# A hybrid decoder layer: input phase and output projection in another order, the second weight difference made in another block

## The chip, the core and the metric

The kernel runs on one core of a Trainium2 chip. The metric is the device time of one execution in microseconds (us). A core has five engines with a queue each: TensorE (PE: matmuls and transposes), VectorE (DVE), ScalarE (ACT), GpSimd (POOL) and SyncE (SP, which here issues DMAs). An engine takes its instructions in the order in which they stand in its queue and waits on semaphores for the other engines and for DMAs.

## The reference, cut to what matters

The program is one layer of a decoder trunk with three gated branches. It computes for 1024 prompt rows and 64 sample rows of 1024 columns:

```python
h = rmsnorm(x, g_pre)
proj = h @ w_in                       # 1024 -> 7 * 512 + 3 * 1024 columns
a      = pool_mix(p_in) * silu(p_gate)            # trailing windows, per-group linear
bconv  = silu(layernorm(dwconv31(c_val * sigmoid(c_glu)))) * silu(c_gate)
cattn  = attention(q, mem_k, mem_v) * silu(x_gate)
br     = einsum('bsnw,nwd->bsnd', stack([a, bconv, cattn]), w_branch)
merged = sum_n sigmoid(merge_logits_n) * br_n     # M, transposed, in the kernel
y      = merged @ w_out
x_new  = x + rmsnorm(y, g_post)
```

Beside it, mem_k and mem_v are `rmsnorm(mem_prompt) @ w_mem_kv` for 256 memory tokens.

## The kernel before

**Numbers.** Matmul operands are pairs of float16 tiles, a high part and a low part. `hilo` (L74) makes them: ScalarE writes the high part (L75) and VectorE or POOL the low part (L77 without a scale, L79 with one). `mm3` (L81) multiplies two pairs in three matmuls (L85, L88, L89).

**Blocks.** Big products use a scheme with seven block products in place of eight. The activation's operands are seven blocks in the tile `BO`, each of four K-tiles: B11, B21, B22 and the sums T1 to T4. The weights are loaded into `raw`, combined (s1 to s4) by accumulating DMAs that POOL issues (L499 to L507), and split into `ws`. Products go to PSUM tiles `pm` and `pb`, four of each.

**Input phase.** `startup` (L236) loads and scales x, turns it by TensorE transposes (`flip`, L225, into `pb`), and splits it. The first half gives B11 and B21. `second_half(k)` (L290) turns K-tile k of the second half, makes the differences `tq` (L292, L295), and splits B12, B22 and T1; behind the four of them T2 is split, then POOL makes the sums for T3 and T4 (L312, L313). In between stand the two first products (`first`, L275), which fill the gates `sg0` with a Sigmoid (L280) as each arrives; the memory tokens' root-mean-squares (L169, L156: a Sqrt at L159 and a Newton step on VectorE, `newton`, L141); their scaling (`mem_kv`, L339); the split of the pooling weights (in `states`); and the splits of s1 and s2 of the first column pair (`prep1`, `prep2` of `pair`, L446). A tile scheduler puts the instructions of each engine in order, by its own estimate of when each can run.

**Middle.** A list of stages holds 7-product pairs for the columns of w_in, the convolution's taps (L715), attention, and `merge` (L1123), which writes the rows of M (L1155, L1157). The gates' evictions are L513, L632 and L660.

**Output projection.** M now is the activation and w_out is split into `BO`. Its 1024 x 1024 are four blocks of four tiles: (0, 0) and (0, 1) in `q` tiles, (1, 0) and (1, 1) in `raw` tiles. `wo_negate` is a ScalarE copy in place (L1213), `wo_add` four accumulating DMAs of 256 KB issued by POOL (L1217), `wo_split` four hi/lo splits. A table, which is in the diff below, hangs them on stages. The first difference (0, 1) + (0, 0) with (0, 1) negated is T1. The second is (1, 1) += (0, 1); it gives T2 and overwrites (1, 1), so it waits until (1, 1) has been split into B22. It is then added to (0, 0) and (1, 0) for T3 and T4.

`pair_of` (L585) runs the seven products of an `out_pair` (L1275): its sums of M are made on POOL (L594, tiles `sr`), split into `ws`, and its evictions are L602. `Rows.part` (L1258) takes a finished half of a row tile: a Square with its sum (L1260) and a product with the norm's weight (L1265); at the second half it forms the root (L1264, L159, Newton), scales and adds x (L1272), and stores the rows.

## Time and profile before

| | us |
|---|---|
| runs, median | 916.86 |
| runs, all | 915.79, 916.86, 920.7 |
| profiled execution | 915.45 |
| its span in the trace | 913.7 |
| TensorE / VectorE busy | 852.5 / 693.6 |
| ScalarE / POOL busy | 462.1 / 319.7 |
| mean granted TensorE clock | 0.975 |

The profile is one execution. Its page gives busy times, 40 slices of the span with the busy share of each engine and the granted TensorE clock in tenths, the chain of work that ended last, and groups of instructions by line and by the program's names (`ws<-raw,ws` writes a `ws` tile from a `raw` and a `ws` tile). Views of the trace give windows, waits with the instruction that ended them, and the timeline of an engine.

### The profile page before, as it was taken

What the parts mean: (1) busy time and instruction counts of PE and PEld (TensorE: products, weight loads), DVE (VectorE), ACT (ScalarE), POOL (GpSimd) and SP (SyncE); (2) the same over time, 40 slices, a digit from 0 to 9 for tenths busy, and PEclk for the clock granted to TensorE, in tenths of its full rate; (3) what the DMA queues carried; (4) which work ended last, traced back from release to release, by engine and by line L of the source; (5) the groups of instructions that cost most, each with busy time, mean ns of one, the idle gap of its engine ahead of it and who ended that gap; (6) DMA issues with size and microseconds to landing.
All of it is one profiled execution on the core that took longest, in us unless ns stands there. A gap on an engine that the chain in (4) does not pass through costs nothing. (4 is left out here: it accounts for less than half of the span.)

```text
span 913.7 us, 15151 instructions
## 1 busy us (share of the span) xinstructions
PE 852.5 (93%) x5765; PEld 458.3 (50%) x5765; DVE 693.6 (76%) x1097; ACT 462.1 (51%) x988; POOL 319.7 (35%) x354
## 2 busy tenths in 40 slices
PE   5869989999999889999989989999999999998986
PEld 3325445545555545555444545555545555544532
DVE  4798599999957799999988777555345543669886
ACT  7767546645653533333445544456345434645542
POOL 1454243344343451211333556511133212346500
PEclk8979999999999999999999999999999999997998
DMA  8625742425566324434343435545654658463142
GB/s 303 170 56 156 202 97 47 92 70 116 120 219 170 93 40 102 95 63 99 84 106 85 94 80 119 119 111 109 132 122 104 119 127 244 124 136 86 70 127 92
DMA packets 101540, 107.42 MB, mean 118 GB/s; under 512 B 5486, under 2 KB 72036, under 8 KB 101452
## 3 DMA queue, kind: packets, MB, share of 16 engines
q1 hardware_dynamic: 82748, 68.24, 23.8%
q0 software_dynamic: 18720, 38.22, 23.6%
q8 instruction: 45, 0.74, 0.3%
q14 instruction: 27, 0.22, 0.1%
HBM read 62.37 MB, written 6.33 MB: 75 GB/s over the span
## 5 line engine op out<-in xcount | busy, mean ns | idle before, releaser
L85 PE MATMUL pm<-BO,ws 128*128 128x512 f16 x836 | 317.8, 382 | 10.2 <-ACT h L513 3.2
L88 PE MATMUL pm<-BO,ws 128*128 128x512 f16 x836 | 319.2, 382 | 1.1 <-DVE BO L77 0.6
L89 PE MATMUL pm<-BO,ws 128*128 128x512 f16 x836 | 317.6, 382 | 1.6 <-DVE ws L79 1.6
L79 DVE SCALAR_TENSOR_TENSOR ws<-raw,ws 128x512 f16<-128x512 f32 x228 | 188.0, 841 | 73.7 <-ACT ws L75 71.9
L88 PEld LDWEIGHTS <-ws 128*128 128x128 f16 x1548 | 148.4, 99 | 128.1 <-issue 21.6
L89 PEld LDWEIGHTS <-ws 128*128 128x128 f16 x1548 | 148.6, 98 | 121.1 <-issue 5.5
L85 PEld LDWEIGHTS <-ws 128*128 128x128 f16 x1548 | 148.1, 99 | 115.2 <-issue 6.9
L75 ACT ACTIVATE ws<-raw 128x512 f16<-128x512 f32 x228 | 137.8, 628 | 126.8 <-PE pm L89 47.7
L715 DVE SCALAR_TENSOR_TENSOR q<-q,cw,q 128x1024 f32<-128x1024 f32 x120 | 167.8, 1407 | 4.0 <-ACT q L712 3.7
L85 PE MATMUL pb<-q,ws 128*128 128x364 f16 (+1 forms) x288 | 92.4, 322 | 2.0 <-DVE q L1155 2.0
L88 PE MATMUL pb<-q,ws 128*128 128x364 f16 (+1 forms) x288 | 92.5, 321 | 0.0
L89 PE MATMUL pb<-q,ws 128*128 128x364 f16 (+1 forms) x288 | 92.5, 321 | 0.0
L499 POOL DMA_DIRECT2D raw<-raw x25 | 21.9, 877 | 198.3 <-ACT raw L498 182.5
L513 ACT ACTIVATE h<-pm 128x512 f32<-128x512 f32 x75 | 44.2, 591 | 49.4 <-PE pm L89 49.3
L1155 DVE SCALAR_TENSOR_TENSOR q<-q,pb 128x364 f32<-128x364 f32 (+1 forms) x72 | 37.3, 526 | 32.7 <-PE pb L89 27.8
L466 DVE SCALAR_TENSOR_TENSOR q<-pm,h 128x512 f32<-128x512 f32 x51 | 34.9, 685 | 29.8 <-PE pm L89 12.8
L506 POOL DMA_DIRECT2D raw<-raw x25 | 21.6, 863 | 75.7 <-DVE ws L79 26.4
L75 ACT ACTIVATE q<-q 128x1024 f16<-128x1024 f32 (+2 forms) x37 | 35.3, 970 | 24.5 <-DVE q L869 10.9
L77 POOL TENSOR_TENSOR q<-q,q 128x1024 f16<-128x1024 f32 (+1 forms) x17 | 36.8, 2175 | 25.8 <-ACT q L75 25.8
L498 ACT ACTIVATE raw<-raw 128x512 f32<-128x512 f32 x50 | 31.0, 625 | 28.7 <-DVE ws L79 28.1
L507 POOL DMA_DIRECT2D raw<-raw x25 | 22.0, 882 | 66.6 <-DVE ws L79 22.1
L85 PE MATMUL pm<-BS,ws 128*128 128x64 f16 x416 | 43.0, 193 | 1.5 <-DVE q L466 1.5
(240 smaller groups left out, 1252.6 us busy)
## 6 DMA issues: line engine op xcount, KB each, us to landing
raw<-in_w_in SPq DMA_DIRECT2D x104, 256.0 KB, 2.9
raw<-raw POOLq DMA_DIRECT2D x104, 256.0 KB, 3.4
q<-in_x_prompt SPq DMA_DIRECT2D x16, 512.0 KB, 9.1
q<-q POOLq DMA_DIRECT2D x14, 544.0 KB, 6.5
raw<-in_w_branch SPq DMA_DIRECT2D x24, 256.0 KB, 3.9
...
```

The costliest lines, as they stand in the source:

```text
L75: nc.scalar.activation(hi, src, AF.Copy, scale=scale)
L77: (eng or nc.vector).tensor_tensor(lo, src, hi, ALU.subtract)
L79: nc.vector.scalar_tensor_tensor(lo, src, scale, hi, ALU.mult, ALU.subtract)
L85: ins = nc.tensor.matmul(out, wh, xh, start=start and j == 0, stop=False, skip_group_check=partial)
L88: nc.tensor.matmul(out, wh, xl, start=False, stop=False, skip_group_check=partial)
L89: nc.tensor.matmul(out, wl, xh, start=False, stop=stop and j == n - 1, skip_group_check=partial)
L466: nc.vector.scalar_tensor_tensor(dst, ps, sc, base, ALU.mult, ALU.add)
L498: nc.scalar.activation(A(1, kh), A(1, kh), AF.Copy, scale=-1.0)
L507: nc.gpsimd.dma_start(out=A(0, 1), in_=A(0, 0), accum_op=ALU.add)
L513: nc.scalar.activation(v[name], ps, AF.Copy, scale=sc)
L715: ins = nc.vector.scalar_tensor_tensor(acc, src, wj, acc, ALU.mult, ALU.add)
L1155: nc.vector.scalar_tensor_tensor(g, g, 1.0, p, ALU.add, ALU.mult)
```

## The change

In the input phase the gates are written with a plain Copy, and one Sigmoid over all 1088 columns of each follows at the end. The memory tokens' squares and roots stay where they were, the rest of their norm is queued behind the last T1 split (`queued`, which hands that split's two instructions to the scheduler as ones to issue after). So are the pooling weights' split and the splits of s1 and s2 of the first pair. `second_half(1)` now stands ahead of `first(1, 0)`.

For w_out the second difference is made in (0, 1): (0, 1) += (1, 1), from stage 4 on, T2 comes from (0, 1), and (0, 1) is added to (0, 0) at stage 6 and to (1, 0) at stage 7. In the row ends, the part behind the second half of a tile becomes `Rows.end`, which is called after the next block's part, and for the last at the end.

```diff
@@ -153,10 +155,16 @@
         nc.vector.scalar_tensor_tensor(r, r, sc, t, ALU.mult, ALU.mult)
         return r
 
-    def rstd_of(ss, inv_n, sc=1.0):
+    def root_of(ss, inv_n):
         p, n = ss.shape
         s = tiny([P, n])[:p]
         nc.scalar.activation(s, ss, AF.Sqrt, scale=inv_n, bias=eps[:p])
+        return s
+
+    def rstd_of(ss, inv_n, sc=1.0, s=None):
+        p, n = ss.shape
+        if s is None:
+            s = root_of(ss, inv_n)
         v = tiny([P, n])[:p]
         nc.vector.tensor_scalar(v, ss, inv_n, EPS, ALU.mult, ALU.add)
         return newton(s, v, (p, n), sc)
@@ -166,11 +174,23 @@
         (eng or nc.sync).dma_start(out=x[:rows], in_=src)
         return x[:rows]
 
-    def rstds(xs):
+    def squares(xs):
         ss = tiny([P, len(xs)])[: xs[0].shape[0]]
         for t, x in enumerate(xs):
             nc.scalar.activation(junk[: x.shape[0]], x, AF.Square, accum_out=ss[:, t : t + 1])
-        return rstd_of(ss, 1.0 / D)
+        return ss
+
+    def rstds(xs):
+        return rstd_of(squares(xs), 1.0 / D)
+
+    behind = []
+
+    def queued():
+
+        es_ = contextlib.ExitStack()
+        for ins in behind:
+            es_.enter_context(tc.issue_after(ins.ins))
+        return es_
 
     BO = cst.tile([P, 7, 2, 4, HALF], F16, name="BO")
     junk = BO[:, 6].rearrange("p a k n -> p (a k n)")[:, : 2 * D].bitcast(F32)
@@ -269,7 +289,8 @@
                 rs_.append(rstds(xt[k + 1 - k // 4 * 2 : k + 3 - k // 4 * 2]))
 
         xs_r = rstds([xs])
-        mem["r"] = rstds(mems)
+        mem["ss"] = squares(mems)
+        mem["s"] = root_of(mem["ss"], 1.0 / D)
         sg0.update({r: Q([P, T]) for r in range(2)})
 
         def first(r, t0, ops):
@@ -277,7 +298,7 @@
             for kh in range(2):
                 w, n = w0[2 * kh + r], ops[kh]
                 mm3(p, [(w[:, 0, k, :], w[:, 1, k, :], n(k)[0], n(k)[1]) for k in range(4)], kh == 0, kh == 1)
-            nc.scalar.activation(sg0[r][:, t0 : t0 + HALF], p, AF.Sigmoid, scale=1.0 / WS)
+            nc.scalar.activation(sg0[r][:, t0 : t0 + HALF], p, AF.Copy, scale=1.0 / WS)
 
         first(0, 0, [lambda k: bo(B11, k), lambda k: bo(B21, k)])
         scale_x(xt[4:6], rs_[0], True)
@@ -294,15 +315,19 @@
             p, gk = flip(k + 4, 1)
             nc.vector.scalar_tensor_tensor(tq[k][:, 1], p, gk, tq[k][:, 0], ALU.mult, ALU.subtract)
             hilo(p, *bo(B22, k), gk)
-            hilo(tq[k][:, 0], *bo(T1, k), -1.0)
+            hi, lo = bo(T1, k)
+            a = nc.scalar.activation(hi, tq[k][:, 0], AF.Copy, scale=-1.0)
+            return a, nc.vector.scalar_tensor_tensor(lo, tq[k][:, 0], -1.0, hi, ALU.mult, ALU.subtract)
 
         second_half(0)
         yield
+        second_half(1)
+        yield
         first(1, 0, [lambda k: bo(B11, k), lambda k: bo(B21, k)])
+        second_half(2)
         yield
-        for k in range(1, 4):
-            second_half(k)
-            yield
+        behind.extend(second_half(3))
+        yield
         for k in range(4):
             hilo(tq[k][:, 1], *bo(T2, k), -1.0)
         for r in range(2):
@@ -329,12 +354,15 @@
             for kh in range(2):
                 w = w0[2 * kh + r]
                 mm3(p[:, r * NS : (r + 1) * NS], [(w[:, 0, k, :], w[:, 1, k, :], BS[:, 0, 4 * kh + k, :], BS[:, 1, 4 * kh + k, :]) for k in range(4)], kh == 0, kh == 1)
-            nc.scalar.activation(sg0[r][:, S:], p[:, r * NS : (r + 1) * NS], AF.Sigmoid, scale=1.0 / WS)
+            nc.scalar.activation(sg0[r][:, S:], p[:, r * NS : (r + 1) * NS], AF.Copy, scale=1.0 / WS)
+            nc.scalar.activation(sg0[r], sg0[r], AF.Sigmoid)
 
     def mem_kv():
         memT = [Q([P, 2, KT // 2, NMEM], F16) for _ in range(2)]
+        with queued():
+            mem["r"] = rstd_of(mem["ss"], 1.0 / D, s=mem["s"])
         for t, m in enumerate(mems):
             nc.vector.tensor_scalar(m, m, mem["r"][:, t : t + 1], None, ALU.mult)
 
@@ -424,7 +452,8 @@
         for g, win in enumerate(WINS):
             for j in range(win - 1):
                 nc.gpsimd.memset(corr[:, g, j : j + 1], float(win) / (j + 1))
-        hilo(pwr, pws[:, 0], pws[:, 1], WS)
+        with queued():
+            hilo(pwr, pws[:, 0], pws[:, 1], WS)
         yield
         nc.sync.dma_start(out=o["conv_s"][0][:, : CB - DS, :], in_=i["state_conv"][0][:, DS:, :])
         nc.sync.dma_start(out=o["pool_s"][0][:, : PB - DS, :], in_=i["state_pool"][0][:, DS:, :])
@@ -473,9 +502,11 @@
                 prep_a11()
 
         def prep1():
-            spl("s1", lambda: v["s1"])
+            with queued() if ahead else contextlib.nullcontext():
+                spl("s1", lambda: v["s1"])
         def prep2():
-            spl("s2", lambda: v["s2"])
+            with queued() if ahead else contextlib.nullcontext():
+                spl("s2", lambda: v["s2"])
         def prep3():
             spl("a12", lambda: A(0, 1))
 
@@ -1222,10 +1253,10 @@
         (-1, lambda: wo_negate(0, 1)),
         (0, lambda: (wo_add((0, 1), (0, 0)), wo_split(B11, 0, 0))),
         (2, lambda: (wo_split(T1, 0, 1, -1), wo_negate(0, 0))),
-        (5, lambda: (wo_split(B21, 1, 0), wo_negate(1, 0))),
-        (6, lambda: (wo_split(B22, 1, 1), wo_add((1, 1), (0, 1)))),
-        (7, lambda: (wo_split(T2, 1, 1), wo_add((0, 0), (1, 1)))),
-        (9, lambda: (wo_split(T3, 0, 0), wo_add((1, 0), (1, 1)))),
+        (4, lambda: (wo_add((0, 1), (1, 1)), wo_split(B21, 1, 0), wo_negate(1, 0))),
+        (6, lambda: (wo_split(B22, 1, 1), wo_add((0, 0), (0, 1)))),
+        (7, lambda: (wo_split(T2, 0, 1), wo_add((1, 0), (0, 1)))),
+        (9, lambda: wo_split(T3, 0, 0)),
         (10, lambda: wo_split(T4, 1, 0, -1)),
     ]:
         stages[last_pair + s][4].append(f)
@@ -1248,6 +1279,12 @@
                 xo[tt] = x_of(tt)
         return f
 
+    ended = []
+
+    def end_rows():
+        while ended:
+            ended.pop(0)()
+
     class Rows:
 
@@ -1259,13 +1296,15 @@
             m, cs = self.m, slice(hf_ * W, (hf_ + 1) * W)
             nc.scalar.activation(half()[:m], ap, AF.Square, scale=sc, accum_out=self.ss[:, hf_ : hf_ + 1])
             self.halves += 1
+            nc.vector.scalar_tensor_tensor(self.y[:, cs], ap, sc, gp[0][:m, cs], ALU.mult, ALU.mult)
             if self.halves == 2:
-                st = tiny([P, 1])[:m]
-                nc.vector.tensor_tensor(st, self.ss[:, 0:1], self.ss[:, 1:2], ALU.add)
-            nc.vector.scalar_tensor_tensor(self.y[:, cs], ap, sc, gp[0][:m, cs], ALU.mult, ALU.mult)
-            if self.halves < 2:
-                return
-            rr, tt = rstd_of(st, 1.0 / D), self.tt
+                ended.append(self.end)
+
+        def end(self):
+            m, tt = self.m, self.tt
+            st = tiny([P, 1])[:m]
+            nc.vector.tensor_tensor(st, self.ss[:, 0:1], self.ss[:, 1:2], ALU.add)
+            rr = rstd_of(st, 1.0 / D)
             dst = o["y_p"][0, tt * P : tt * P + m, :] if tt < S // P else o["y_s"].rearrange("b s d -> (b s) d")
             for hf_ in range(2):
                 cs = slice(hf_ * W, (hf_ + 1) * W)
@@ -1284,7 +1323,11 @@
             return of(r).y[:, c0 : c0 + HALF]
 
         def block(r, c0, ap, scale):
+            mine = ended[:]
             of(r).part(c0 // HALF, ap, scale or 1.0)
+            for f in mine:
+                ended.remove(f)
+                f()
 
         pair_of(lambda r, kh: [M[4 * kh + k][:, (t + 4 * r) * P : (t + 4 * r + 1) * P] for k in range(4)],
                 dest, block, t == 0)
@@ -1327,6 +1370,7 @@
     after(samples_turn)
     out_pair(2)
     out_pair(3)
+    after(end_rows)
     at = len(stages) - 29
     for s, tts in ((-1, (0, 4)), (5, (8,)), (7, (1, 5)), (14, (2, 6)), (21, (3, 7))):
         stages[at + s][4].append(load_x(*tts))
```

Lines of the changed kernel stand further down: L79 becomes L81, L77 becomes L79, L292 L313, L339 L367, L594 L625, L602 L633, L1161 L1192, L1217 L1248, L1264 L1306, L1265 L1299, L1272 L1311.

VectorE in the input phase, the order before, from the scaling of the sample rows on. `t_279` is the memory tokens' root, `q_104` and `q_106` the tokens, `ws_648` to `ws_663` weight splits:

```order
L79 SCALAR_TENSOR_TENSOR ws_648<-raw_126,ws_648 128x512
L79 SCALAR_TENSOR_TENSOR ws_651<-raw_642,ws_651 128x512
L79 SCALAR_TENSOR_TENSOR ws_654<-raw_645,ws_654 128x512
L292 SCALAR_TENSOR_TENSOR q_328<-pb_332,g_pre,q_136 128x512
L145 RECIPROCAL t_283<-t_279 128x2
L295 SCALAR_TENSOR_TENSOR q_328<-pb_340,g_pre,q_328 128x512
L150 TENSOR_TENSOR t_285<-t_283 128x2
L79 SCALAR_TENSOR_TENSOR q_326<-pb_332,g_pre,q_326 128x512
L151 TENSOR_TENSOR t_285<-t_285,t_281 128x2
L79 SCALAR_TENSOR_TENSOR BO<-q_328,BO 128x512
L152 TENSOR_SCALAR t_285<-t_285 128x2
L292 SCALAR_TENSOR_TENSOR q_329<-pb_394,g_pre,q_137 128x512
```

The same place in the order of the change, where `q_319` and `q_320` are the differences of K-tiles 0 and 1:

```order
L313 SCALAR_TENSOR_TENSOR q_319<-pb_323,g_pre,q_136 128x512
L316 SCALAR_TENSOR_TENSOR q_319<-pb_331,g_pre,q_319 128x512
L313 SCALAR_TENSOR_TENSOR q_320<-pb_341,g_pre,q_137 128x512
L81 SCALAR_TENSOR_TENSOR q_317<-pb_323,g_pre,q_317 128x512
L320 SCALAR_TENSOR_TENSOR BO<-q_319,BO 128x512
L316 SCALAR_TENSOR_TENSOR q_320<-pb_349,g_pre,q_320 128x512
L81 SCALAR_TENSOR_TENSOR BO<-pb_331,g_pre,BO 128x512
```

Three weight splits and the Newton step have gone from between the differences, and the second flip's difference follows the first one's at once. The weight splits and the Newton step now stand behind the last T1 split, and the tokens' scaling behind the T3 and T4 low parts.

POOL at the output projection, the order before, from the second sum of M on (`q_7984`, `q_8000`, `q_8019`, `q_8039` hold the K-tiles of blocks (0, 0) and (0, 1) of w_out, `raw_8060` to `raw_8139` those of (1, 0) and (1, 1)):

```order
L594 TENSOR_TENSOR sr_8372<-sr_8367,q_3277 128x128
L594 TENSOR_TENSOR sr_8401<-q_4006,sr_8372 128x128
L594 TENSOR_TENSOR sr_8401<-q_4027,sr_8372 128x128
L594 TENSOR_TENSOR sr_8436<-q_3225 128x128
L594 TENSOR_TENSOR sr_8436<-q_3277 128x128
L594 TENSOR_TENSOR sr_8436<-q_3704 128x128
L594 TENSOR_TENSOR sr_8436<-q_3728 128x128
L1217 DMA raw_8060<-q_7984 128x512
L1217 DMA raw_8090<-q_8000 128x512
L1217 DMA raw_8106<-q_8019 128x512
L1217 DMA q_7984<-raw_8060 128x512
L1217 DMA raw_8060<-raw_8060 128x512
```

The same place in the change, with tile numbers higher by two:

```order
L625 TENSOR_TENSOR sr_8374<-sr_8369,q_3279 128x128
L1248 DMA q_7986<-raw_8062 128x512
L1248 DMA q_8002<-raw_8092 128x512
L1248 DMA q_8021<-raw_8108 128x512
L1248 DMA q_7986<-q_7986 128x512
L1248 DMA q_8041<-raw_8141 128x512
L1248 DMA q_8002<-q_8002 128x512
L625 TENSOR_TENSOR sr_8403<-q_4008,sr_8374 128x128
L625 TENSOR_TENSOR sr_8403<-q_4029,sr_8374 128x128
L1248 DMA q_8021<-q_8021 128x512
L625 TENSOR_TENSOR sr_8438<-q_3227 128x128
```

The second difference now stands directly behind that sum, ahead of six others, and all twelve transfers stand ahead of the later sums.

VectorE within the second pair of row tiles, before. L1264, L161, L145 and L148 to L153 are the root of a finished row tile, `h_9245` a block's combination:

```order
L148 SCALAR_TENSOR_TENSOR t_9153<-t_9151,t_9149 128x1
L1272 SCALAR_TENSOR_TENSOR q_9027<-q_9027,t_9105,q_8932 128x512 x2
L152 TENSOR_SCALAR t_9153<-t_9153 128x1
L1265 SCALAR_TENSOR_TENSOR q_9161<-pb_9163,q_8421 64x512
L1264 TENSOR_TENSOR t_9178<-t_9162 64x1
L1265 SCALAR_TENSOR_TENSOR q_9161<-pb_9171,q_8421 64x512
L153 SCALAR_TENSOR_TENSOR t_9151<-t_9151,t_9153 128x1
L602 SCALAR_TENSOR_TENSOR h_9245<-pm_9232,h_9221 128x512
```

And in the change, where `h_9215` is that combination:

```order
L1299 SCALAR_TENSOR_TENSOR q_9147<-pb_9149,q_8423 64x512
L1299 SCALAR_TENSOR_TENSOR q_9147<-pb_9157,q_8423 64x512
L155 SCALAR_TENSOR_TENSOR t_9137<-t_9137,t_9139 128x1
L633 SCALAR_TENSOR_TENSOR h_9215<-pm_9202,h_9191 128x512
L81 SCALAR_TENSOR_TENSOR ws_9486<-sr_9345,ws_9486 128x128 x4
L1311 SCALAR_TENSOR_TENSOR q_9013<-q_9013,t_9137,q_8918 128x512 x2
```

The scaling of the finished rows has moved from ahead of the combination to behind it.

More of the change, by code (lines that the diff above doesn't have):

```diff
@@ L2 @@
+import contextlib
 import concourse.bass as bass
```

## The prediction

> **What bounds the kernel now.** First the page's engine line and its slices. TensorE is busy 93% of the span, so its own work is the floor, and only what it loses can be won.
>
> ```profile
> PE 852.5 (93%) x5765; PEld 458.3 (50%) x5765; DVE 693.6 (76%) x1097; ACT 462.1 (51%) x988; POOL 319.7 (35%) x354
> ...
> PE   5869989999999889999989989999999999998986
> ...
> PEclk8979999999999999999999999999999999997998
> ```
>
> A slice is 22.8 us. The dips to read are the third slice (46 to 69 us, clock 7) and the 37th (822 to 845, clock 7). The first lies in the input phase, the second at the start of the output projection, where the change works. The windows view in steps of 5 us gives the loss there. Its columns are length, then busy time and count on PE, PEld, DVE, ACT and POOL, then granted clock, DMA share, GB/s.
>
> ```profile
> 40.00:45.00 5.00, 1.50 (x7) 0.68 (x7) 2.93 (x7) 4.96 (x8) 2.82 (x4) 0.97 0.50 91
> 45.00:50.00 5.00, 2.60 (x9) 1.26 (x8) 5.00 (x7) 4.72 (x10) 3.12 (x3) 0.50 0.62 136
> 50.00:55.00 5.00, 3.74 (x14) 1.30 (x13) 5.00 (x6) 1.72 (x3) 2.13 (x3) 0.84 0.54 117
> 55.00:60.00 5.00, 2.21 (x8) 0.83 (x8) 5.00 (x7) 2.07 (x4) 2.78 (x2) 0.84 0.11 20
> 60.00:65.00 5.00, 4.11 (x16) 1.61 (x14) 5.00 (x8) 4.55 (x9) 2.97 (x2) 0.50 0.01 2
> ```
>
> ```profile
> 820.00:825.00 5.00, 2.24 (x8) 0.74 (x6) 3.11 (x5) 1.48 (x4) 2.56 (x6) 0.80 1.08 278
> 825.00:830.00 5.00, 2.90 (x20) 1.20 (x18) 5.00 (x6) 2.88 (x7) 5.00 (x11) 0.84 1.06 216
> 830.00:835.00 5.00, 4.15 (x41) 2.76 (x42) 5.00 (x12) 3.66 (x14) 2.81 (x7) 0.50 0.04 7
> 835.00:840.00 5.00, 5.00 (x76) 3.34 (x74) 4.04 (x17) 3.76 (x19) 0.63 (x2) 0.84 0.02 3
> ```
>
> Busy time times clock is the work at full clock. From 40 to 65 us that is 1.46 + 1.30 + 3.14 + 1.86 + 2.06 = 9.8 us in 25: **15.2 us are lost**. From 820 to 840 it is 1.79 + 2.44 + 2.08 + 4.20 = 10.5 in 20: **9.5 us are lost**. From 45 to 65 us VectorE (DVE) is busy all of 20 us: it makes the operands that TensorE waits for. In the second stall the DMA share is above 1 until 830 us, and VectorE and ScalarE are not full at first: there transfers bound.
>
> The page's rule on its clock is borne out by these rows: 830 to 835 us has 83% of busy time at clock 0.50, after 10 us half idle. The Trainium skill ("TensorE: Matmul & The Clock Gate", "What's actually happening") says that an idle window of about 3.4 us halves the clock and a busy one of that length restores it. By it, a stall that is only cut into small gaps would keep the half clock; that is weighed with the rivals.
>
> **The input phase.** The timeline view shows what VectorE spends there on work that nothing near it needs (start, length, engine, line, operation, and idle time before it with its releaser).
>
> ```profile
> 39.12 0.60 ACT L280 ACTIVATE q<-pm 128x512 f32<-128x512 f32 x1
> 39.74 1.28 ACT L159 ACT_TABLE_LOAD   x1
> ```
>
> ```profile
> 41.36 0.17 DVE L145 RECIPROCAL t<-t 128x2 f32<-128x2 f32 x1 [2.00 <-ACT t L159]
> ...
> 44.31 3.01 DVE L152 TENSOR_SCALAR t<-t 128x2 f32<-128x2 f32 x1
> ...
> 49.88 1.40 DVE L339 TENSOR_SCALAR q<-q,t 128x1024 f32<-128x1024 f32 x2
> 51.21 1.28 DVE L79 SCALAR_TENSOR_TENSOR ws<-raw,ws 128x512 f16<-128x512 f32 x2
> ...
> 67.21 1.75 DVE L79 SCALAR_TENSOR_TENSOR pws<-q,pws 128x512 f16<-128x512 f32 x1
> ...
> 70.45 1.75 DVE L77 TENSOR_TENSOR BO<-h,BO 128x512 f16<-128x512 f32 x1
> ```
>
> Moved behind the operands' splits are: the wait for the memory tokens' root behind table loads (2.00); that Newton chain (five operations, of 0.17 and about 0.15, about 0.75; the 3.01 is a collision, priced below); the memory scaling (1.40); two weight splits (1.28); the pooling weights' split (0.68 alone, by the mean of such splits below). Sum 2.00 + 0.75 + 1.40 + 1.28 + 0.68 = **6.1 us** by which VectorE reaches the last T2 split (70.45) earlier. The two flips that now stand together give it work at once, so I take the whole. The three ScalarE table loads become one with the deferred sigmoids; beyond the 2.00 I cost this at nothing: ScalarE is 2.07 and 1.72 busy in two of the 5 us windows. If that cover were gone the two new sigmoids over 1088 columns, by the 0.60 of one over 512 some 1.3 each, would cost up to 2.6.
>
> What is moved must still be done:
>
> ```profile
> 80.00:85.00 5.00, 5.00 (x72) 3.08 (x69) 2.23 (x5) 1.98 (x5) 0.89 (x2) 1.00 0.95 285
> ```
>
> Here VectorE has 2.77 us free and the moved 4.1 us (6.1 less the wait) do not quite fit; the first split of the next pair (s3) and the memory transposes come late. I take 1.0 back, between nothing and 4.1. **Net 5.1.**
>
> The unknown is contention of VectorE with POOL (GpSimd), shown by groups of the same operation. First POOL and VectorE from 43 to 74 us, last VectorE from 786 to 806 us, where POOL scarcely computes beside it (count, then busy us and mean ns).
>
> ```profile
> L77 POOL TENSOR_TENSOR BO<-h,BO 128x512 f16<-128x512 f32 x4 | 6.2, 1555 | 3.8 <-ACT BO L75 3.8
> L312 POOL TENSOR_TENSOR h<-q,q 128x512 f32<-128x512 f32 x4 | 6.2, 1545 | 0.2
> L313 POOL TENSOR_TENSOR h<-q,q 128x512 f32<-128x512 f32 x4 | 5.7, 1432 | 1.7 <-PE pb L1345 1.0 <-DVE BO L77 0.6
> ```
>
> ```profile
> L79 DVE SCALAR_TENSOR_TENSOR BO<-q,BO 128x512 f16<-128x512 f32 x8 | 9.1, 1134 | 0.0
> L77 DVE TENSOR_TENSOR BO<-h,BO 128x512 f16<-128x512 f32 x4 | 5.2, 1290 | 0.0
> ```
>
> ```profile
> L79 DVE SCALAR_TENSOR_TENSOR BO<-q,BO 128x512 f16<-128x512 f32 x4 | 2.7, 688 | 0.7 <-ACT BO L75 0.7
> ```
>
> The excess is 8 x (1.13 - 0.69) = 3.6, 4 x (1.29 - 0.69) = 2.4, 2.9 on the 0.15 of the Newton operation, and 1.1 on the pooling split: **10.0 us** beside 18.1 us of POOL work. The change leaves these twelve POOL operations as they are, so I keep 10.0. The ends: all 18.1 block, which costs 8.1 more and makes the part 5.1 - 8.1 = -3.0; or as few collide as let it gain 9.
>
> The Trainium skill ("SBUF: State Buffer", "Who interferes with whom") speaks against the change here: a VectorE operation with two SBUF inputs and a POOL operation that reads SBUF shut each other out for their whole length. The rows agree in kind (1134 against 688 ns). By it a denser VectorE row would meet more of the 18.1 us, up to the end of -3.0.
>
> **The output projection.** The timeline of TensorE, POOL, VectorE (the last row of M) and ScalarE, then the landing times of the accumulating transfers (L1217), then windows ahead of the stall:
>
> ```profile
> 823.00 0.21 PE L85 MATMUL pb<-ws,BO 128*128 128x64 f16 x1 [2.76 <-ACT ws L75]
> ```
>
> ```profile
> 789.99 0.46 POOL L594 TENSOR_TENSOR sr<-sr,q 128x128 f32<-128x128 f32 x1
> ...
> 807.17 2.68 POOL L1217 DMA_DIRECT2D raw<-q  x3 [11.77 <-DVE BO L79]
> ...
> 822.44 0.88 POOL L1217 DMA_DIRECT2D q<-raw  x1 [3.56 <-DMA raw<-q]
> ```
>
> ```profile
> 817.66 0.52 DVE L1157 TENSOR_TENSOR q<-q,q 128x360 f32<-128x360 f32 x1
> ```
>
> ```profile
> 831.55 0.63 ACT L75 ACTIVATE BO<-raw 128x512 f16<-128x512 f32 x1 [0.29 <-DMA raw<-raw]
> ```
>
> ```profile
> DMA to landing us min/median/max: 3.2/7.9/13.6
> ```
>
> ```profile
> 790.00:795.00 5.00, 5.00 (x71) 3.55 (x70) 4.01 (x7) 4.52 (x10) 4.50 (x7) 1.00 0.30 106
> 795.00:800.00 5.00, 5.00 (x30) 2.72 (x28) 3.99 (x14) 4.28 (x17) 0.40 (x1) 1.00 0.00 0
> 800.00:805.00 5.00, 5.00 (x28) 2.55 (x27) 0.15 (x2) 1.04 (x4) 0.00 (x0) 1.00 0.00 0
> ```
>
> POOL stands 11.77 us until block (1,1) has been split into B22, since that block is then overwritten. From 807.17 to the last landing's split on ScalarE at 831.55 the twelve transfers take 24.4 us beside the loads of x. The sums of M (L594) are queued behind the waiting transfer of 822.44 on POOL, TensorE waits for those sums' splits, and ScalarE, in order, for each landing.
>
> In the new order the first of the twelve stands right behind the sum that ran at 789.99 before, since block (0,1) is free once T1 is split. So the chain starts some 16 us earlier, in a stretch whose DMA share is 0.30, 0.00 and 0.00. Even with three dependent rounds at the median of 7.9 it ends near 790.5 + 23.7 = 814, before TensorE runs dry at 820. The count of transfers is the same, so nothing is added. What is late next: the M sums now stand behind more transfers, and the last M row is there only at 817.66 as before. I leave 3.0 of the 9.5 for that, bounded by nothing left (gain 9.5) and by a longer wait than now (loss, below). **Gain 6.5.**
>
> **The row ends.** Here TensorE waits 2.69 us for a combination (L602) that stands behind the scaling of finished rows.
>
> ```profile
> 879.17 0.38 PE L85 MATMUL pm<-BO,ws 128*128 128x512 f16 x1 [2.69 <-DVE t L161]
> ```
>
> ```profile
> 875.73 1.41 DVE L1272 SCALAR_TENSOR_TENSOR q<-q,t,q 128x512 f32<-128x512 f32 x2
> ...
> 904.91 0.15 DVE L145 RECIPROCAL t<-t 128x1 f32<-128x1 f32 x1
> ```
>
> With the end of a row queued behind the next block, the 1.41 us and its small Newton operations go from in front of that combination, others take their place: I take **1.0**, between 0 and 2.7. At the very end nothing hides the deferral: three Newton operations of 0.15 now follow the last combination: **-0.5**, between 0 and -1.
>
> **Sum.** 5.1 + 6.5 + 1.0 - 0.5 = 12.1. The profiled execution took 915.45 us (span 913.7), so 903.35; the runs' median, 916.86, is 1.4 above it, and half of that puts the forecast at **904.0**. Its own range is 898 to 908.5. In the long middle, from 130 to 530 us, both queues are shuffled a little; that is 2 or 3 us of unknown sign, inside this range.
>
> **The rivals.** One half per cent (4.6 us) is about what a measurement of this kernel can tell from no change.
> - The denser VectorE queue collides with POOL so that the input phase gains nothing: 915.45 - 6.5 - 1.0 + 0.5 = 908.45. For it the 10.0 us of excess, against it the unchanged twelve operations. 0.13.
> - The output stall only breaks into gaps and TensorE stays at half clock. A stretch such as 825 to 835, with work 2.44 + 2.08 = 4.5 at 7.05 busy, loses 2.5 to the clock alone; with two such stretches and 2 to 3 idle the part gains only 2: 915.45 - 5.1 - 2 - 1.0 + 0.5 = 907.85. For it the 0.50 at 830 to 835. 0.12. It is the result that the rule of the Trainium skill's page "TensorE: Matmul & The Clock Gate" would give for a stall in pieces.
> - The change doesn't do what it says: both stalls are moved, not removed, since TensorE does the same work and VectorE, full at both ends, ends last anyway: 911 to 920. 0.15.
> - Slower, by one mechanism: ScalarE works in order, and the splits of T2 and T3 now stand at about 795 us ahead of the evictions (L513) and gates (L660) that free TensorE's PSUM tiles. If landings need the maximum of 13.6 us in two rounds, to 790.5 + 27 = 817, ScalarE is held, TensorE idles in the merge some 17 us less the 9.5 that it would have lost later, and loses 3 more to half clock while it refills: 915.45 - 4.1 (other parts, input phase at 3.6) + 7.5 + 3 = 922. It decides from landings over about 10 us; against it, the free DMA queues at 795 to 805. 0.06.
> - Better than 898, both parts near their upper ends (9 and 9.5): 0.04.
>
> The forecast keeps 0.50. Faster by over 0.5% means under 912.3: 0.50 + 0.13 + 0.12 + 0.04 and 0.03 of the third rival, 0.82. Within: the rest of that rival, 0.12. Slower: 0.06. The range 897 to 915 leaves out the 0.06, about 0.08 of the third rival above 915 and most of the 0.04.
>
> **What would show it.** In the changed profile: no root wait of 2 us on VectorE near 41 us, the last T2 split near 64 us in place of 70.45, and work at full clock from 40 to 65 near 15 in place of 9.8. POOL's first second-difference transfer near 791 in place of 807, ScalarE's last T4 split before 820 in place of 831.55, and the loss from 820 to 840 (shifted by the earlier gain) near 3. The wait of 2.69 near 879 under 2. Wrong would be: mean split times above 1134 ns at the start; idle TensorE between 790 and 815; clock 0.5 in the output projection's first 10 us.

## The result and the profile after

The changed kernel took **903.88 us** (median of four runs, 900.14 to 904.58); the kernel before took 916.33 us beside it (913.23 to 920.7). The ratio is **0.9856, with a 95% interval of 0.9826 to 0.9886**. The profiled execution took 903.34 us with a span of 901.6. The forecast was 904.0. The total was right, but several of its terms were not: the row ends came out three times their size, the w_out part gave nothing beside the others, and a stretch priced at nothing gave as much as the input phase.

First the changed kernel's page: busy time of the engine, then the slices of TensorE and of its granted clock.

```profile
PE 847.4 (94%) x5765; PEld 456.8 (51%) x5765; DVE 688.4 (76%) x1097; ACT 462.4 (51%) x988; POOL 314.0 (35%) x354
...
PE   5979999999999879899999989999999999898995
...
PEclk8889999999999989999999999999999999999998
```

A slice is 22.5 us now. Both dips that the prediction named, at slices 3 and 37, are shallower, but a new one stands at slice 35 (766 to 789 us), just ahead of the old second dip. The windows view of the changed kernel (length, busy time and count on PE, PEld, DVE, ACT and POOL, granted clock, DMA share, GB/s), input phase first:

```profile
25.00:30.00 5.00, 4.48 (x11) 1.57 (x11) 5.00 (x10) 2.82 (x5) 1.48 (x1) 0.50 0.84 232
...
40.00:45.00 5.00, 5.00 (x28) 2.79 (x27) 5.00 (x6) 1.96 (x4) 3.81 (x4) 1.00 0.30 53
45.00:50.00 5.00, 2.65 (x17) 1.53 (x15) 3.73 (x6) 2.87 (x7) 4.46 (x4) 1.00 0.69 154
50.00:55.00 5.00, 3.07 (x14) 1.38 (x13) 5.00 (x8) 4.80 (x10) 2.42 (x2) 0.55 0.00 0
55.00:60.00 5.00, 5.00 (x20) 2.09 (x19) 5.00 (x8) 4.47 (x9) 3.69 (x3) 0.76 0.01 2
60.00:65.00 5.00, 4.22 (x23) 2.03 (x22) 5.00 (x9) 2.27 (x5) 2.81 (x4) 1.00 0.01 3
65.00:70.00 5.00, 3.53 (x37) 1.89 (x36) 4.89 (x11) 3.08 (x7) 2.10 (x3) 1.00 0.42 75
```

Busy time times clock is again the work at full clock. From 40 to 65 us it is 5.00 + 2.65 + 1.69 + 3.80 + 4.22 = 17.4 us in place of 9.8. To 70 us the loss is 9.1, where it was 15.3 (the 15.2 of the prediction, which ends at 65 us, and 0.1 more). But from 25 to 30 us TensorE now runs 4.48 us at clock 0.50, so 2.8 are lost in this execution. The kernel before lost nothing there:

```profile
25.00:30.00 5.00, 5.00 (x25) 2.16 (x23) 5.00 (x10) 2.73 (x6) 1.84 (x2) 1.00 0.78 246
```

The same view of the changed kernel at the output projection:

```profile
785.00:790.00 5.00, 2.25 (x14) 1.15 (x12) 2.04 (x3) 3.99 (x9) 3.91 (x7) 1.00 0.86 155
...
800.00:805.00 5.00, 3.79 (x21) 1.85 (x19) 1.79 (x4) 2.15 (x6) 0.00 (x0) 1.00 0.59 145
...
810.00:815.00 5.00, 4.02 (x31) 2.00 (x30) 5.00 (x18) 0.63 (x2) 1.91 (x4) 1.00 0.09 35
815.00:820.00 5.00, 2.77 (x17) 0.89 (x14) 4.31 (x13) 2.38 (x10) 4.00 (x7) 0.85 0.00 0
820.00:825.00 5.00, 4.41 (x47) 2.33 (x46) 5.00 (x14) 2.77 (x14) 3.78 (x9) 0.81 0.01 2
```

The losses are 2.75, 1.21, 0.98, 2.65 and 1.43, **9.0 us, against 9.5 before**. They have moved, and they have hardly shrunk. Why the first of them is there is read in two engines' timelines (start, length, engine, line, operation, and in brackets the idle time before it with its releaser). TensorE of the changed kernel:

```profile
788.85 0.38 PE L87 MATMUL pm<-BO,ws 128*128 128x512 f16 x1 [2.75 <-ACT h L544]
```

ScalarE of the changed kernel, at the same time and later:

```profile
785.89 0.63 ACT L77 ACTIVATE BO<-q 128x512 f16<-128x512 f32 x1 [3.06 <-DMA q<-raw]
786.42 0.61 ACT L691 ACTIVATE q<-q 128x512 f32<-128x512 f32 x1
787.16 0.63 ACT L77 ACTIVATE BO<-q 128x512 f16<-128x512 f32 x1
787.70 0.61 ACT L1244 ACTIVATE raw<-raw 128x512 f32<-128x512 f32 x1
788.22 0.58 ACT L544 ACTIVATE h<-pm 128x512 f32<-128x512 f32 x1
...
802.85 0.63 ACT L77 ACTIVATE BO<-raw 128x512 f16<-128x512 f32 x1 [3.33 <-DMA raw<-q]
...
806.54 0.62 ACT L77 ACTIVATE BO<-raw 128x512 f16<-128x512 f32 x1
...
815.95 0.70 ACT L77 ACTIVATE ws<-q 128x128 f16<-128x128 f32 x2 [5.33 <-DVE q L1188]
```

TensorE needs a free PSUM tile for its products. The eviction that frees it (L544) stands four places behind a split of T2 that waits 3.06 us for an accumulating transfer. ScalarE takes its queue in order, so the eviction waits for a landing with which it has nothing to do. This is the "slower" rival's mechanism, at 2.75 us of TensorE. The row at 802.85 does the same through VectorE: its low part of that split waits 3.21 us for the high part, the row of M queued behind it (L1186) comes late, and TensorE idles 1.21 us for that row at 804.71. The last row shown is the other loss: ScalarE stands 5.33 us until a row of M is there, 9 us after the last T4 split (806.54).

To follow where the time goes, the same instruction is compared between two traces: by how many us does each eviction start earlier than in the profiled execution before? Columns are times in the trace of before; the evictions of `pm` into `h` are taken up to 798 us, the combinations of the out pairs behind that (the last at 905).

| kernel | 115 | 249 | 372 | 407 | 483 | 784 | 798 | 837 | 905 |
|---|---|---|---|---|---|---|---|---|---|
| the change | 3.8 | 9.5 | 10.9 | 5.5 | 11.8 | 10.3 | 3.2 | 14.0 | 12.7 |
| e1: input phase alone | 5.7 | 11.5 | 12.7 | 7.3 | 13.7 | 12.0 | 11.8 | 14.0 | 13.2 |
| e2: w_out alone | -1.2 | -0.8 | -1.3 | -1.3 | -1.4 | -2.2 | -8.6 | 2.1 | 0.1 |
| e3: row ends alone | -1.2 | -1.2 | -2.7 | -2.7 | -3.2 | -3.5 | -4.3 | -2.6 | -0.1 |
| e8: input phase, row ends | 4.3 | 10.3 | 11.4 | 6.1 | 12.6 | 11.8 | 10.9 | 13.2 | 16.2 |
| e9: the change, evictions first | 5.2 | 10.4 | 11.6 | 6.3 | 12.7 | 11.2 | 11.4 | 16.9 | 17.6 |

e2 and e3 have before's program until about 760 us and still lie 1.2 to 3.5 behind it: so far do two single traces differ by themselves. The change's lead falls from 10.3 to 3.2 between 784 and 798 us, while M is merged, and rises again where the old stall stood. e1 keeps its 12.0 there. TensorE itself loses only 4.2 us from 785 to 805 by the windows, so part of this fall is the late place of that one eviction and not lost time.

### The profile page after: what moved, and what is told of

Same layout as the page of the kernel before. It is cut to its first block, busy times and chain, and to the rows that moved or that the text cites. A ratio compares the mean times of both kernels' runs of the same rounds, so it can differ in the third digit from the quotient of the medians.

```text
span 901.6 us, 15160 instructions
## 1 busy us (share of the span) xinstructions
PE 847.4 (94%) x5765; PEld 456.8 (51%) x5765; DVE 688.4 (76%) x1097; ACT 462.4 (51%) x988; POOL 314.0 (35%) x354
## 4 chain that ended last, share of the span: by engine, by line
PE 36%; DVE 6%; DMA 4%; POOL 2%; issue 2%; ACT 1%; DVEq 0%; POOLq 0%; ACTq 0%
PE pm L87 9%; PE pm L91 9%; PE pm L90 9%; PE pb L90 3%; PE pb L91 3%; PE pb L87 3%; DVE ws L81 2%; DMA q<-q 1%; DMA raw<-raw 1%; DMA raw<-q 1%; POOL q L1248 1%; DVE q L1311 1%; POOL sr L625 1%; POOL q L1024 0%; DVE BO L81 0%
## 5 line engine op out<-in xcount | busy, mean ns | idle before, releaser
L87 PE MATMUL pm<-BO,ws 128*128 128x512 f16 x836 | 319.1, 383 | 11.6 <-ACT h L544 5.9
L81 DVE SCALAR_TENSOR_TENSOR ws<-raw,ws 128x512 f16<-128x512 f32 x228 | 189.3, 846 | 64.7 <-ACT ws L77 62.9
L77 ACT ACTIVATE ws<-raw 128x512 f16<-128x512 f32 x228 | 138.4, 626 | 120.5 <-PE pm L91 50.3
L746 DVE SCALAR_TENSOR_TENSOR q<-q,cw,q 128x1024 f32<-128x1024 f32 x120 | 165.2, 1383 | 5.5 <-ACT q L743 5.1
L544 ACT ACTIVATE h<-pm 128x512 f32<-128x512 f32 x75 | 44.2, 591 | 56.2 <-PE pm L91 56.1
L1186 DVE SCALAR_TENSOR_TENSOR q<-q,pb 128x364 f32<-128x364 f32 (+1 forms) x72 | 37.1, 526 | 26.3 <-PE pb L91 26.3
L77 ACT ACTIVATE q<-q 128x1024 f16<-128x1024 f32 (+2 forms) x37 | 35.5, 975 | 27.2 <-DVE q L900 13.5
L87 PE MATMUL pm<-BS,ws 128*128 128x64 f16 x416 | 43.7, 193 | 3.1 <-DVE q L495 3.1
L90 PE MATMUL pm<-BS,ws 128*128 128x64 f16 x416 | 43.4, 193 | 1.3 <-DVE BS L79 1.3
```

Of the source, the lines that this page charges most:

```text
L77: nc.scalar.activation(hi, src, AF.Copy, scale=scale)
L81: nc.vector.scalar_tensor_tensor(lo, src, scale, hi, ALU.mult, ALU.subtract)
L87: ins = nc.tensor.matmul(out, wh, xh, start=start and j == 0, stop=False, skip_group_check=partial)
L90: nc.tensor.matmul(out, wh, xl, start=False, stop=False, skip_group_check=partial)
L544: nc.scalar.activation(v[name], ps, AF.Copy, scale=sc)
L746: ins = nc.vector.scalar_tensor_tensor(acc, src, wj, acc, ALU.mult, ALU.add)
```

## The experiments

All ratios are to the kernel before in the same session, with a 95% interval.

**e1, e2, e3: each part alone.** e1 is the change with the old table for w_out and the old row ends. e2 is the kernel before with the new table, e3 the kernel before with `Rows.end`:

```diff
 e1, against the change
-        (4, lambda: (wo_add((0, 1), (1, 1)), wo_split(B21, 1, 0), wo_negate(1, 0))),
+        (5, lambda: (wo_split(B21, 1, 0), wo_negate(1, 0))),
...
-            if self.halves == 2:
-                ended.append(self.end)
 e2, against before
-        (6, lambda: (wo_split(B22, 1, 1), wo_add((1, 1), (0, 1)))),
+        (4, lambda: (wo_add((0, 1), (1, 1)), wo_split(B21, 1, 0), wo_negate(1, 0))),
...
 e3, against before
+            if self.halves == 2:
+                ended.append(self.end)
```

> Only the input phase of the change; output projection and row ends as before. By the prediction's terms: 5.1 us faster, all of it won between 40 and 75 us. By the account made from the two traces (the same evictions, L513, set side by side: 3.8 us ahead at 115 us, 8.9 at 250 to 330, 10.3 from 585 to 784): about 10 us faster, with over half of it won in the middle, from 130 to 540 us, by another order there.

> Only the second difference of w_out in the other block. By the prediction's term: 6.5 us faster. By the traces' account (the lead goes from 10.3 us ahead of the output projection to about 12.9 at the first row tiles behind it): 2 to 3 us faster, with TensorE idle some 2.8 us before an eviction (L513) near 799 us and still losing 4 to 5 us at full clock between 820 and 840.

> Only the row ends deferred. By the prediction's terms: 0.5 us faster (1.0 won near 879, 0.5 lost at the end). By the traces' account: the wait of 2.69 us near 879 is gone, but its gain is given back between 855 and 870, so from 0 to 1 us faster, and a tail about 0.5 us longer behind the last matmul. Rival: 2.2 us faster, the whole wait less the tail.

e1 took 905.58 us, 0.9877 [0.9847, 0.9906]: 11.3 us gained, twice the 5.1 of the prediction. e2 took 912.31, 0.9959 [0.9935, 0.9982]: 3.7 us, between 1.7 and 6.0. e3 took 914.05, 0.9965 [0.9943, 0.9986]: 3.2 us, between 1.3 and 5.2. In e2, without any input phase edit, TensorE waits in the merge for an eviction as in the change:

```profile
800.65 0.41 PE L85 MATMUL pm<-BO,ws 128*128 128x512 f16 x1 [1.99 <-ACT h L513]
```

**e4: the change once more**, as it is, in the session of e1 to e3.

> The changed kernel once more, as the sum to hold the parts against, and for a second profile of it. If the parts are independent its gain is the sum of the other three: 12.1 us by the prediction's terms (5.1 + 6.5 + 0.5), about 12 to 13 by the traces' account (10 + 2.5 + 0 to 1). If the clock of 0.50 from 20 to 30 us in the first profile belongs to one execution and not to the order of the work, this profile shows a clock as before there (0.58, then 1.00).

903.59 us, 0.9849 [0.9819, 0.9879], a gain of 13.9. The three parts alone add up to 18.2, so some 4 us of them are lost together. The second question has its answer too: in e4 the clock is 0.97 from 25 to 30 us, with 3.36 us busy, so 1.7 are lost there and not 2.8. The half clock in that window belongs to one execution; the rest, idle time of TensorE, belongs to the order. The last section shows the rows.

**e5: two taps back.** In the pooling step of the middle, two convolution taps on VectorE stood between three operations that lead to a product. In the input phase's new order the scheduler places them elsewhere, though no edit touches them. e5 is e1 with these two taps tied into their old place:

```diff
+                n = len(taps)
+                with tc.issue_after(mixed[n - 110].ins) if 110 <= n < 112 else contextlib.nullcontext():
+                    ins = nc.vector.scalar_tensor_tensor(acc, src, wj, acc, ALU.mult, ALU.add)
+                taps.append(ins)
```

> The input-phase part alone (as in e1), with two of the convolution's taps put back where they stand before the change, between the three VectorE steps of the first pooling group near 450 us; five rows of VectorE's order and two of ScalarE's differ from e1, nothing else. If the unexpected gain in the middle is those two taps, TensorE idles 1.3 and 2.1 us there again with half clock after it: 4 to 5 us slower than e1, the loss from 440 to 470 us about 6 in place of 0.7. Rival, the gain there comes from elsewhere: no slower than e1 by more than 1 us.

VectorE before (L715 are the taps, L998, L999 and L77 the steps), then TensorE, which waits for the last of them:

```profile
458.04 0.43 DVE L998 TENSOR_TENSOR q<-q,corr 128x1 f32<-128x1 f32 x1 [3.00 <-POOL q L993]
...
458.62 1.28 DVE L715 SCALAR_TENSOR_TENSOR q<-q,cw,q 128x1024 f32<-128x1024 f32 x1
459.81 1.22 DVE L999 SCALAR_TENSOR_TENSOR q<-q,q 128x1024 f32<-128x1024 f32 x1
...
461.55 1.28 DVE L715 SCALAR_TENSOR_TENSOR q<-q,cw,q 128x1024 f32<-128x1024 f32 x1
463.35 1.22 DVE L77 TENSOR_TENSOR q<-q,q 128x1024 f16<-128x1024 f32 x1
```

```profile
464.62 0.46 PE L88 MATMUL pb<-q,pws 128*128 128x364 f16 x1 [2.07 <-DVE q L77]
```

The same place in the changed kernel, VectorE (the steps L1030 and L79, with no tap between them) and then TensorE:

```profile
450.76 1.22 DVE L1030 SCALAR_TENSOR_TENSOR q<-q,q 128x1024 f32<-128x1024 f32 x1
...
453.16 1.23 DVE L79 TENSOR_TENSOR q<-q,q 128x1024 f16<-128x1024 f32 x1
```

```profile
454.44 0.31 PE L90 MATMUL pb<-q,pws 128*128 128x364 f16 x1 [0.84 <-DVE q L79]
```

And in e5, TensorE with the taps back:

```profile
456.49 0.31 PE L90 MATMUL pb<-q,pws 128*128 128x364 f16 x1 [2.20 <-DVE q L79]
```

The wait of 2 us is back. Between 440 and 470 us e5 loses 4.0 us of work at full clock, where e1 loses 0.7 and the kernel before 5.5. e5 took 908.23 us, 0.9918 [0.9889, 0.9947], so 2.7 more than e1 by the medians, 3.8 by the ratios, whose intervals still touch, and 3.3 by the traces. That is less than the 4 to 5 us expected, but far from the rival's 1. Two taps out of 120 are worth more than half of the 5.1 that was given to the whole input phase.

**e6: evictions ahead of the T2 and T3 splits.** The change, with these splits tied behind the last eviction of the merge:

```diff
+            kepts.append(nc.scalar.activation(v[name], ps, AF.Copy, scale=sc))
...
+    def wo_split_late(n, kh, ch):
+        with tc.issue_after(kepts[-1].ins):
+            wo_split(n, kh, ch)
...
-        (7, lambda: (wo_split(T2, 0, 1), wo_add((1, 0), (0, 1)))),
-        (9, lambda: wo_split(T3, 0, 0)),
+        (7, lambda: (wo_split_late(T2, 0, 1), wo_add((1, 0), (0, 1)))),
+        (9, lambda: wo_split_late(T3, 0, 0)),
```

> The changed kernel with the splits of T2 and T3 of w_out queued on ScalarE behind the last pair's evictions (L544). If ScalarE, held by the landing of the second difference ahead of these evictions, is what idles TensorE 2.75 us at 788.85 us, that idle is gone and the kernel is 2 to 3 us faster than the changed one (e4). Rival, the end of M sets the start of the output projection anyway: the idle is gone at 788 and comes back between 810 and 825, and the time is that of e4 within 1 us.

903.02 us, 0.9858 [0.9829, 0.9886]: no gain over the change. The idle is gone at 788 us, as both forecasts said, but it came back at 791, which neither said. So these splits alone don't cost the time. ScalarE and TensorE of e6 show why:

```profile
791.35 0.71 ACT L77 ACTIVATE ws<-sr 128x128 f16<-128x128 f32 x2 [4.93 <-POOL sr L626]
...
794.04 0.57 ACT L545 ACTIVATE h<-pm 128x512 f32<-128x512 f32 x1
```

```profile
794.67 0.38 PE L87 MATMUL pm<-BO,ws 128*128 128x512 f16 x1 [3.36 <-ACT h L545]
```

The next item in ScalarE's queue took the place of the first. It is the split of a sum of M, which POOL makes behind the transfers that were moved ahead of it.

**e7, e10, e11: pieces of the input phase.** Each is e1 with one piece undone: nothing queued (Newton step, pooling weights and weight splits in their old places), the sigmoids in place, `first(1, 0)` ahead of `second_half(1)`:

```diff
 e7
-        with queued():
-            hilo(pwr, pws[:, 0], pws[:, 1], WS)
+        hilo(pwr, pws[:, 0], pws[:, 1], WS)
...
 e10
-            nc.scalar.activation(sg0[r][:, t0 : t0 + HALF], p, AF.Copy, scale=1.0 / WS)
+            nc.scalar.activation(sg0[r][:, t0 : t0 + HALF], p, AF.Sigmoid, scale=1.0 / WS)
...
 e11
+        first(1, 0, [lambda k: bo(B11, k), lambda k: bo(B21, k)])
+        yield
         second_half(1)
         yield
-        first(1, 0, [lambda k: bo(B11, k), lambda k: bo(B21, k)])
```

> The input-phase part without its queueing behind the last T1 split: the sigmoids deferred and the second flip ahead, but the Newton step, the scaling, the pooling split and the pair's splits where the scheduler puts them; from 310 us on VectorE's order is that of before. By the prediction's terms only the 2.0 of the wait for the root is won in the input phase. The stall at 460 us stays (about 6 us lost from 440 to 470). So 2 to 5 us faster than before, against about 11 for e1. Rival, the queueing is worth nothing and the order in the middle all: input phase as in e1 (5 to 6 us ahead at 115 us).

> The input-phase part with each Sigmoid in its old place (three table loads on ScalarE near 35 to 45 us again), flips and queueing as in e1. The prediction puts 2.0 of its 6.1 us on the wait behind those loads: then about 2 us slower than e1, the lead at 115 us (L513) about 2.4 in place of 4 to 5.7. Rival: with the Newton step queued behind the T1 splits nothing near waits for the root, and the loads are hidden: within 1 us of e1.

> The input-phase part with the second product (first(1, 0)) back ahead of the second flip. In the changed order TensorE waits 1.0 us at 25.5 us for a split that the second product's matmuls would have covered, and stays at clock 0.50 to 30 us: about 2.5 us lost from 25 to 30 that the kernel before does not lose. If the second product's place makes that, it is not lost here; the flips then come later, which by the prediction costs part of the 6.1. The place of one tap (of two in e5) costs 1.5 to 2 more. So the loss from 25 to 30 under 0.5 us, that from 40 to 70 us 2 to 5 more than in e1 (7.7 there by its windows 45 to 70), and the time 0 to 5 us slower than e1. Rival, the half clock there is chance: loss of about 2.5 here too.

| kernel | us | ratio | loss 25 to 30 | loss 40 to 70 | lead at 115 | lead at 585 |
|---|---|---|---|---|---|---|
| before | | | 0 | 15.3 | | |
| e1 | 905.58 | 0.9877 [0.9847, 0.9906] | 1.6 | 9.3 | 5.7 | 12.0 |
| e7 | 911.46 | 0.9942 [0.9922, 0.9962] | 3.0 | 9.4 | 0.2 | 3.8 |
| e10 | 911.86 | 0.9940 [0.9919, 0.9960] | 3.0 | 9.0 | -3.5 | 5.0 |
| e11 | 907.57 | 0.9900 [0.9870, 0.9929] | 0 | 14.0 | 3.2 | 9.3 |

e11 tells two things at once. The second product's place is what wins the 40 to 70 us stretch (14.0 against 9.3). It is also what costs the stretch from 25 to 30: put back, the loss there is gone. In time, e11 is 2.0 us slower than e1 by the medians, and the intervals overlap. e7 and e10 keep the gain of the 40 to 70 us stretch and lose time elsewhere. e7 gained 5.3 us, and the stall near 460 us stayed (5.8 lost from 440 to 470), as expected. e10 is 6.3 us slower than e1, which neither its forecast (2) nor its rival (1) gave. Its table loads (at 34, 36 and 45 us) leave the windows from 30 to 40 us full and the loss from 40 to 70 at 9.0, so the loss isn't there. Behind them TensorE waits again for an eviction in ScalarE's queue, behind a split that waits for a transfer; the rest of its loss was not traced. ScalarE and then TensorE of e10:

```profile
79.31 0.63 ACT L77 ACTIVATE ws<-raw 128x512 f16<-128x512 f32 x1 [2.97 <-DMA raw<-in_w_in]
...
82.90 0.59 ACT L543 ACTIVATE h<-pm 128x512 f32<-128x512 f32 x1
```

```profile
83.54 0.38 PE L87 MATMUL pm<-BO,ws 128*128 128x512 f16 x1 [2.56 <-ACT h L543]
```

So neither run prices its piece cleanly: the scheduler gives every variant an order of its own further on.

**e8: the change with the old w_out table**, so input phase and row ends only.

```diff
-        (4, lambda: (wo_add((0, 1), (1, 1)), wo_split(B21, 1, 0), wo_negate(1, 0))),
-        (6, lambda: (wo_split(B22, 1, 1), wo_add((0, 0), (0, 1)))),
+        (5, lambda: (wo_split(B21, 1, 0), wo_negate(1, 0))),
+        (6, lambda: (wo_split(B22, 1, 1), wo_add((1, 1), (0, 1)))),
...
```

> The change without its part on w_out. If the parts add up: 11.3 (e1) and 3.2 (e3), 14 to 15 us faster, as fast as the whole change (13.9) or faster, since the w_out part's gain of 2 to 3 overlaps with that of the row ends. If the w_out part brings what it brought alone (3.7): 3 to 4 us slower than the whole change.

902.53 us, 0.9857 [0.9824, 0.9890], as fast as the whole change. The w_out part, worth 3.7 us alone, is worth nothing beside the other two. Without it e8 still has the old stall; TensorE waits 4 us for the low half of a split of M's rows:

```profile
815.80 0.21 PE L90 MATMUL pb<-ws,BO 128*128 128x64 f16 x1 [3.97 <-DVE ws L81]
```

**e9 and e12: no eviction held.** e9 is e6 with the splits of the first out pair's sums also behind the last eviction. e12 is this second tie alone on e8, so without the w_out part and without e6's tie on the T2 and T3 splits:

```diff
-            for k, y in enumerate(x):
-                hilo(y, w[:, 0, k], w[:, 1, k], MS)
+            with tc.issue_after(kepts[-1].ins) if late else contextlib.nullcontext():
+                for k, y in enumerate(x):
+                    hilo(y, w[:, 0, k], w[:, 1, k], MS)
```

> The changed kernel, with the splits of T2 and T3 and all splits of the first output pair's sums queued on ScalarE behind the last evictions (L544), since in e6 ScalarE stood 4.93 us at a sum of POOL ahead of one. If these holds are what the w_out part paid for its early transfers, TensorE idles under 1 us between 780 and 800 us (2.8 to 3.4 in the changed kernel and e6), and the kernel is 2 to 4 us faster than the changed one: 899 to 901. Rival, the sums on POOL, now all behind the transfers, come later and the stall at 815 to 825 grows by as much: no faster than e8 (902.5).

> The kernel of e8 (input phase and row ends, w_out as before) with the splits of the first output pair's sums queued behind the last evictions, as in e9. It tells whose gain e9 has. If it is that of w_out's part, which pays only once no eviction waits: this kernel is as e8, 902 to 903. Rival, the order of those splits is itself the gain and w_out's part is worth nothing: 897 to 899, as e9.

e9 took **898.09 us (896.69 to 900.12), 0.9795 [0.9767, 0.9823]**. It beats both kernels, the change by 5.8 and 5.5 us (its medians were 903.88 and 903.59). At 916.33 the ratio is a gain of 18.8 us, near the 18.2 of the three parts alone. That they meet so closely isn't a proof that the parts add: each gain is uncertain by about 2 us or more, and the 3.7 of e2 already had an eviction held (1.99 us). e12 took 901.91, 0.9854 [0.9826, 0.9882], as e8. So the tie gains nothing without the w_out part, and e9, with both ties and that part, is 3.8 us faster than e12: what they free is that part's gain. The windows of e9, ahead of the stall and in it:

```profile
785.00:790.00 5.00, 5.00 (x31) 2.87 (x30) 2.48 (x4) 3.11 (x7) 5.00 (x8) 1.00 1.13 201
...
805.00:810.00 5.00, 4.28 (x35) 2.01 (x33) 5.00 (x20) 1.45 (x5) 4.45 (x3) 1.00 0.51 200
810.00:815.00 5.00, 2.76 (x13) 0.91 (x11) 4.31 (x11) 2.57 (x9) 3.69 (x8) 0.94 0.00 0
815.00:820.00 5.00, 4.62 (x21) 2.06 (x21) 5.00 (x12) 2.12 (x10) 4.78 (x11) 0.50 0.00 0
```

The merge is full (5.00 from 785 to 790, where the change has 2.25). What is left stands behind 805: 0.72 + 2.41 + 2.69, and 0.65 behind 820, 6.5 us. From 810 us on VectorE is 4.31 to 5.00 busy and the DMA share is 0.00, and TensorE's waits there (1.22 us at 813.19, 1.22 at 815.38) end with the splits of the last rows of M and of their sums: these bind now, not the transfers.

## Why the prediction was right, and where it was not

**The input phase, net 5.1: right in size, but by luck, since its parts were wrong.** From 40 to 70 us the loss fell from 15.3 to 9.1, by 6.2, close to the 6.1 that was written down. At 115 us the change leads by 3.8 and e1 by 5.7, or some 5 to 7 against the kernels that have before's program there (-1.2). The rows that were promised are there. No wait for the memory tokens' root stands near 41 us. The split quoted as "the last T2 split" at 70.45 was really one of T3 or T4 (it reads `h`); the last of T2 stood at 69.84. VectorE of the changed kernel has four weight splits and then the two at

```profile
61.15 3.26 DVE L81 SCALAR_TENSOR_TENSOR ws<-raw,ws 128x512 f16<-128x512 f32 x4
...
65.06 1.72 DVE L81 SCALAR_TENSOR_TENSOR BO<-q,BO 128x512 f16<-128x512 f32 x1
...
68.58 0.68 DVE L79 TENSOR_TENSOR BO<-h,BO 128x512 f16<-128x512 f32 x1
```

so T2 is earlier by 4.8 and the other by 1.9, not by the 6 that the sign asked for. Three steps failed.

- The sum took the moved work to stand behind the last T2 split. It is queued behind the last T1 split: five weight splits (one of 1.65 us at 59.27 and the four above, 4.9 us together) now stand ahead of the last T2 split, where the sum counted two of them, 1.28 us, as gone.
- The sum gave the gain to that moved work and to the 2.00 of the root behind table loads. With nothing queued (e7) the stretch loses 9.4, and with the sigmoids and their loads in place (e10) 9.0, both about as e1. What e11 shows to carry the stretch is the order of product and flips.
- The first product, now without the second behind it, was not looked at. TensorE waits there, and from 25 to 30 us it loses 1.6 to 3.0 us in the profiles of this order, 2.8 in that of the changed kernel (e11: nothing).

**Contention, kept at 10.0: about right.** Groups of VectorE in the changed kernel from 36 to 70 us (count, then busy us and mean ns):

```profile
L320 DVE SCALAR_TENSOR_TENSOR BO<-q,BO 128x512 f16<-128x512 f32 x4 | 6.6, 1639 | 0.0
L81 DVE SCALAR_TENSOR_TENSOR BO<-q,BO 128x512 f16<-128x512 f32 x4 | 3.9, 968 | 0.0
L79 DVE TENSOR_TENSOR BO<-h,BO 128x512 f16<-128x512 f32 x4 | 3.1, 778 | 1.2 <-ACT BO L77 1.2
```

The twelve splits take 13.6 us, a mean of 1.13; before it was 9.1 + 5.2 = 14.3 and 1.19. The eight of T1 and T2 became dearer (1.31 against 1.134, the sign that was to be wrong) and the four of T3 and T4 cheaper (0.778 against 1.290). Counted as in the prediction, with 1.75 for two slow weight splits and 1.1 for a Newton operation, the excess is 8.2 us. A denser VectorE row didn't meet more of POOL's work, so the rival that rested on the Trainium skill ("SBUF — State Buffer", "Who interferes with whom") didn't come; that the two engines shut each other out is borne out by the 1639 ns beside 688.

**The middle, "2 or 3 us of unknown sign": wrong, it gave 6.** Between 115 and 784 us the lead grows from 3.8 to 10.3, in e1 from 5.7 to 12.0. Most of the net gain comes early: to 249 us the lead of the change is already 9.5 and that of e1 11.5, and it grows there in e5 (4.4 to 9.8) and e7 (0.2 to 5.0) as well. TensorE's longest wait in this stretch, before and then in e1:

```profile
135.28 0.28 PE L89 MATMUL pb<-q,q 128*128 128x256 f16 x1 [3.04 <-DVE q L79]
```

```profile
127.73 0.28 PE L91 MATMUL pb<-q,q 128*128 128x256 f16 x1 [0.20 <-DVE q L81]
```

Just ahead of it, before, a weight split on VectorE took 4.35 us (at 128.95) while POOL worked beside it; in e1 that split took 0.67 and the tap behind it 3.18. So VectorE's operations seem to meet those of POOL otherwise there; no run isolates this step. From 249 to 784 us the steps have both signs (in the change -5.4 between 372 and 407, +6.3 to 483) and come to 0.8 in the change and 0.5 in e1. In e5, with the taps back, they come to -2.5. So the taps are worth about 3 us of the 6, and without them the later middle would have lost time. Which moved rows make the other steps was not tried.

**The output projection, 6.5: wrong.** The transfers went as forecast. POOL issued the first three here, at the 791 of the forecast less the lead of 10.3:

```profile
780.52 2.78 POOL L1248 DMA_DIRECT2D q<-raw  x3
```

and the last T4 split stood at 806.54, well before 820. The step that failed is "what is late next ... I leave 3.0". Left were 9.0: 4.0 in the merge (2.75 and 1.21) and 5.1 at M's last rows. The merge's part was named, as the slower rival, but with a wrong condition: it was to decide "from landings over about 10 us". The landings of the changed kernel:

```profile
DMA to landing us min/median/max: 3.6/5.7/10.2
```

They were shorter than before (7.9 in the median), and the hold came all the same: the landing that held the T2 split took about 5 us (issued at 780.52, the split began at 785.89). The split is queued ahead of the eviction by 4 places, and any wait of it is passed on. The size was 4.0 us of TensorE, not 17. e6, e9 and e12 show the mechanism from three sides: take away one held item and the next one holds (3.36); take both away and 5.5 us come back; without the w_out part the tie that was tried frees nothing.

**The row ends, 1.0: the mechanism right, the size too small.** e3 gained 3.2 alone, and e8 3.0 on top of e1 by the medians (1.8 by the ratios). No wait of TensorE for a combination near 866 to 880 us is left, so all of the 2.69 went. **The tail, -0.5:** the time behind the last matmul rose from 8.4 to 9.0, as forecast.

**The half clock.** That rival's price (907.85) was for a stall in pieces. The pieces came: clock 0.85 and 0.81 in the changed kernel from 815 to 825, 0.50 in e9 from 815 to 820. The w_out part won even less than the 2 us it was given there, yet the time was not that rival's, since the middle made up for it. So the forecast of 904.0 was met by luck, through errors of opposite sign: -6.5 for w_out, +6 for the middle, and about +2 for the row ends against the loss from 25 to 30.
